# A block inverse from 32-blocks: the three terms of a float16 pair stacked along the contraction

## The chip, the cores and the metric

The kernel runs on one core of a Trainium2 chip. The metric is the device time of one execution in microseconds (us). TensorE (PE) multiplies matrices and writes to PSUM; VectorE (DVE), ScalarE (ACT) and GpSimd (POOL) work element by element; SyncE (SP) issues most DMA transfers, in the order of its own queue. Each engine takes its instructions in a fixed order, which is set when the kernel is compiled.

## The reference

One layer of a hybrid backbone for 2048 sample tokens and 128 context tokens with D = 1024. Three branches work on one input projection; the change lies in the first, a gated delta rule in both directions. Cut to what matters:

```python
def gated_delta_chunked(q, k, v, g, beta, s0):
    ...
    m = eye + bc[..., :, None] * jnp.einsum('bnhik,bnhjk->bnhij', kc, kc) * dec_strict
    rhs = jnp.concatenate([vc * bc[..., None], kc * (bc * jnp.exp(gam))[..., None]], axis=-1)
    sol = lax.linalg.triangular_solve(m, rhs, left_side=True, lower=True, unit_diagonal=True)
    ...
    def step(s, inp):
        u0_, w_, qk_, qg_, kd_, gl_ = inp
        u = u0_ - jnp.einsum('bhck,bhkv->bhcv', w_, s)
        o = jnp.einsum('bhck,bhkv->bhcv', qg_, s) + jnp.einsum('bhij,bhjv->bhiv', qk_, u)
        s = gl_[..., None, None] * s + jnp.einsum('bhck,bhcv->bhkv', kd_, u)
        return s, o
```

The other two branches (a spatial gating unit and a Fourier mix), the gates, the merge and the output projection are matrix products around it. The result holds the tokens of both groups and the final states of the context.

## The kernel before

**Numbers.** Float32 values are held as pairs of float16, a high and a low part. A product of two pairs takes three matmuls, high by high, high by low and low by high (`mm3`, L163; each goes through `mm`, L160, so almost every matmul of the profile stands at L161).

**Chunks.** The kernel uses chunks of 128 tokens, 17 of them: chunk 16 is the context, 0 to 15 the sample. For each chunk, direction and head (H = 4) a unit triangular matrix of 128 by 128 is inverted. `prep` (L652) makes the products of a chunk: it reads the rows of q, k and v (`rows`, tiles kq and qr; one chunk ahead), normalizes them (`norm`: squares on ACT, a scale and a power on POOL), and writes the off-diagonal matrix `n16` as a pair to DRAM (`nD`), and its four diagonal blocks of 32 by 32 through POOL copies (L712) to `ndD`. Stores are issued one step late (`late`).

**Inverses of the 32-blocks.** `base_inverse` (L736) inverts the diagonal blocks of four chunks (a group) at once, by 31 steps on DVE (L759, L760), and writes each inverse and its transpose side by side as float32 to `eD` (L770).

**From 32 to 128.** `level` (L777) is run once for each of the 17 chunks in each direction, 34 times. It loads `n` (tile sn) and the inverses (tile e), splits the inverses to float16 pairs (`ec`, L790 and L791) and spreads them over block-diagonal tiles R16 (the inverse) and T16 (its transpose) with a mask on POOL (L797). Then two levels of block products follow: n times T16, masked (`q32`, L808) and split to Q; Q with R16 and R16 with Q; the results go to R16 and T16 with minus signs (L824 to L830); n times T16 again (L834, mask L837), then Q with R16 (L843). Each of the five products has three terms for four heads, 12 matmuls, 60 in all. Almost all use 128 rows and columns of the array, with zeros in most blocks.

**The scan.** `scan_dir` (L878) runs the chunks of one direction in order; each step needs R of its chunk, which `level` of that chunk makes during the step before. Both are generators. `attend` gives a chunk's output and `finish` the second direction's.

**The order.** The matmuls of the other branches and of the merge are the main program; after each block `Pace.tick` runs some steps of the delta generator (`delta`, L996), by a quota of time per step (QUOTA 1.6, in the scan SCAN 2.7). At the end of the second merge the rest is drained (L1327). A scheduler then orders the instructions of each engine.

**Weights.** Projection weights come in blocks of 128 columns (`wlist`). `fetch` and `weight_step` (L260 to L281) read them and convert them to pairs, some steps per tick; `getw(n, ahead)` gives the next and asks for the following.

The lines that load and spread a level's operands:

```python
        e32 = sb(dq, [P, H, 2, 32], "e32")
        SY.dma_start(e32.rearrange("p h w c -> p h (w c)"), eD[g][d, :, ci])
        ...
        for which, dst in ((0, R16), (1, T16)):
            for l in range(2):
                G.tensor_tensor(dst[:, l].rearrange("p h a b c -> p h (a b) c"), wide(ec[:, :, which ^ d, l, :]), bm, ALU.mult)
```

Of the kernel before, what the change touches and what calls it, by code (L numbers as in the profile page):

```python
# [20 lines left out]
P = 128  # L21
# [90 lines left out]
def hybrid_flow_kernel(ctx: ExitStack, tc: tile.TileContext, x_prompt, x_sample, state_delta, c, c_ctx, ln_g, w_ada,  # L112
# [56 lines left out]
    def rsqrt(out, ss, mul, w):  # L169
        G.tensor_scalar(out, ss, mul, EPS, ALU.mult, ALU.add)  # L170
        G.tensor_tensor(out, out, mhalf.to_broadcast([P, w]), ALU.pow)

    def scales(ss, pl, tag):

        ps = bank(ps_x, [P, 1])
        sb16 = sb(pl, [P, 1], tag + "b", BF16)
        V.tensor_copy(sb16, ss)  # L177
        mm(ps, ones16, sb16)
# [16 lines left out]
    def converting(w, st, nkt, cols=P, hi=None, lo=None, tag="w", bufs=5):  # L195
# [12 lines left out]
        s, inv = scales(ss, wp, "wsc")  # L208
# [43 lines left out]
    v4, vfilled = [], [0]  # L252
    wdone, wnext, wread, wlate, bwp, wsteps = [], [0], [], [0], [], []

    def read_next():
        if len(wread) < min(len(wdone) + 2, len(wlist)):
            src, nkt, tag, bufs = wlist[len(wread)]
            wread.append(read_w(src, nkt))

    def weight_step():  # L260

        if wsteps:
            if next(wsteps[0], 1):
                wsteps.pop(0)
                wlate[0] = 3
        else:
            wlate[0] -= 1
            if wlate[0] <= 0:
                read_next()

    def fetch(upto):
        while len(wdone) < min(upto, len(wlist)):
            src, nkt, tag, bufs = wlist[len(wdone)]
            if tag == "b" and not bwp:
                return
            if len(wread) == len(wdone):
                while wsteps:
                    weight_step()
                read_next()
            wdone.append(_W())  # L280
            wsteps.append(converting(wdone[-1], wread[len(wdone) - 1], nkt, tag=tag, bufs=bufs))  # L281
# [127 lines left out]
    with tc.issue_after(last_ada.ins):  # L409
        fetch(2)  # L410
# [174 lines left out]
    for ct in range(12):  # L585
        w = getw(1, 2)
# [40 lines left out]
    eD = [dram(f"ei{g}", [2, P, len(ts), H, 64]) for g, ts in enumerate(GROUPS)]  # L627
# [10 lines left out]
    def rows(part, t):  # L638
        x = sb(d2, [P, H, P], "kq" if part else "qr", bufs=3 if part else 1)
# [5 lines left out]
    def late(dst, src):  # L645

        if owed:
            SY.dma_start(*owed.pop())
        if dst is not None:
            owed.append((dst, src))  # L650

    def prep(g, ci, t, nxt, held):  # L652
# [11 lines left out]
        def norm(ps, i):  # L664
# [3 lines left out]
            G.tensor_scalar(ss[:, i, :], ss[:, i, :], EPS, None, ALU.add)  # L668
# [10 lines left out]
        yield 1  # L679
        A.activation(tok[:, 1, :], turned(2), AF.Copy, scale=us)  # L680
# [18 lines left out]
        more(0, lambda: rows(0, nxt))  # L699
# [7 lines left out]
        for d in range(2):  # L707
# [3 lines left out]
            for B in range(4):  # L711
                G.tensor_copy(nd[32 * B:32 * B + 32, d], h3(n_)[32 * B:32 * B + 32, :, 32 * B:32 * B + 32])  # L712
# [3 lines left out]
            late(nD[d][t], n16)  # L716
# [19 lines left out]
    def base_inverse(g):  # L736
# [26 lines left out]
        both = XB.rearrange("p (j w c) -> p j w c", j=32, w=2)  # L763
        V.tensor_copy(both[:, :, 1, :], E.rearrange("p (i j) -> p j i", j=32))
        A.copy(both[:, :, 0, :], b3(E))
        yield 1
        for d in range(2):
            for B in range(4):
                p0_ = d * 64 + B * 16
                SY.dma_start(eD[g][d, 32 * B:32 * B + 32].rearrange("j t h c -> (t h) j c"),  # L770
                             both[p0_:p0_ + nb].rearrange("p j w c -> p j (w c)"))
# [3 lines left out]
    odd = [False]  # L775

    def level(d, t):  # L777
        odd[0] = not odd[0]
        ps_l = ps_x if odd[0] else ps_lev
# [6 lines left out]
        R16 = sb(dq, [P, 2, H, 2, 2, 32], "R16", F16, bufs=2)  # L786
        R = R16.rearrange("p l h a b c -> p l (h a b c)")
        yield R
        ec = sb(dq, [P, H, 2, 2, 32], "ec", F16)
        A.activation(ec[:, :, :, 0, :], e32, AF.Copy, scale=FS)  # L790
        V.scalar_tensor_tensor(ec[:, :, :, 1, :], e32, FS, ec[:, :, :, 0, :], ALU.mult, ALU.subtract)  # L791
        T16 = sb(dq, [P, 2, H, 2, 2, 32], "T16", F16, bufs=2)
        bm = K["bm"].rearrange("p (o b x) -> p o b x", o=1, x=1).to_broadcast([P, H, 4, 32])
        wide = lambda t_: t_.rearrange("p h (o c) -> p h o c", o=1).to_broadcast([P, H, 4, 32])
        for which, dst in ((0, R16), (1, T16)):
            for l in range(2):
                G.tensor_tensor(dst[:, l].rearrange("p h a b c -> p h (a b) c"), wide(ec[:, :, which ^ d, l, :]), bm, ALU.mult)  # L797
        yield R
        b0 = d
        nl = lambda h: (n_[:, 0, hs(h)], n_[:, 1, hs(h)])  # L800
        sub = lambda t_, h, b: (t_[:, 0, h, :, b, :], t_[:, 1, h, :, b, :])
        ps = bank(ps_l, [P, H, 64])
        for h in range(H):
            mm3(ps[:, h].rearrange("p (a c) -> p a c", a=2), nl(h), sub(T16, h, b0))
        Q = sb(dq, [P, 2, H, 64], "Q", F16, bufs=2)
        m1 = K["m1f" if d == 0 else "m1b"].rearrange("p (o a x) -> p o a x", o=1, x=1).to_broadcast([P, H, 2, 32])
        f = sb(dq, [P, H, 64], "q32", bufs=2)
        V.tensor_tensor(f.rearrange("p h (a c) -> p h a c", a=2), ps.rearrange("p h (a c) -> p h a c", a=2), m1, ALU.mult)  # L808
        A.activation(Q[:, 0], f, AF.Copy, scale=1.0 / FS)
        V.scalar_tensor_tensor(Q[:, 1], f, 1.0 / FS, Q[:, 0], ALU.mult, ALU.subtract)  # L810
        yield R
        ps12 = bank(ps_l, [P, 2, H, 2, 32])
        ps1, ps2 = ps12[0:64, 0], ps12[:, 1]
# [4 lines left out]
        yield R  # L818
        a0 = d
        rows = lambda a, b: slice(64 * a + 32 * b, 64 * a + 32 * b + 32)  # L820
        for a in (1 - a0, a0):
            ra = rows(a, b0)
            src = ps1[32 * a:32 * a + 32, :, a, :]
            A.activation(R16[ra, 0, :, a, 1 - b0, :], src, AF.Copy, scale=-1.0 / FS)  # L824
            V.scalar_tensor_tensor(R16[ra, 1, :, a, 1 - b0, :], src, -1.0 / FS, R16[ra, 0, :, a, 1 - b0, :], ALU.mult, ALU.subtract)
        a = a0
        ra = rows(a, 1 - b0)
        src = ps2[ra, :, a, :]
        A.activation(T16[ra, 0, :, a, b0, :], src, AF.Copy, scale=-1.0 / FS)
        V.scalar_tensor_tensor(T16[ra, 1, :, a, b0, :], src, -1.0 / FS, T16[ra, 0, :, a, b0, :], ALU.mult, ALU.subtract)  # L830
        half = lambda t_, h, a_: (t_[:, 0, h, a_].rearrange("p b c -> p (b c)"), t_[:, 1, h, a_].rearrange("p b c -> p (b c)"))
        ps = bank(ps_l, [P, H, 64])
        for h in range(H):
            mm3(ps[:, h], nl(h), half(T16, h, a0))  # L834
        Q = sb(dq, [P, 2, H, 64], "Q", F16, bufs=2)
        f = sb(dq, [P, H, 64], "q32", bufs=2)
        V.tensor_scalar(f, ps, K["m2f" if d == 0 else "m2b"], None, ALU.mult)  # L837
        A.activation(Q[:, 0], f, AF.Copy, scale=1.0 / FS)
        V.scalar_tensor_tensor(Q[:, 1], f, 1.0 / FS, Q[:, 0], ALU.mult, ALU.subtract)
        yield R  # L840
        ps = bank(ps_l, [64, H, 64])
        for h in range(H):
            mm3(ps[:, h], (Q[:, 0, h, :], Q[:, 1, h, :]), half(R16, h, 1 - a0))  # L843
        top = [R16[64 * a0:64 * a0 + 64, l, :, 1 - a0].rearrange("p h b c -> p h (b c)") for l in range(2)]
        A.activation(top[0], ps, AF.Copy, scale=-1.0 / FS)
        V.scalar_tensor_tensor(top[1], ps, -1.0 / FS, top[0], ALU.mult, ALU.subtract)
        yield R

# [29 lines left out]
    def scan_dir(d):  # L878
        order = [16] + (list(range(16)) if d == 0 else list(range(15, -1, -1)))
        lev = level(d, order[0])  # L880
        R = next(lev)
        for _ in range(5):
            yield 1
        for R in lev:
            yield 1
            yield 1
        S = S16 = held = None
        for s_, t in enumerate(order):
            nlev = level(d, order[s_ + 1]) if s_ < 16 else iter(())
            R2 = next(nlev, None)  # L890
# [21 lines left out]
            if held is not None:  # L912
                yield from attend(d, *held)
# [543 lines left out]
```

## Time and profile before

| | |
|---|---|
| time, median of three runs | 2273.56 us (2272.32 to 2273.77) |
| the profiled execution | 2270.88 us, of which span 2269.1 us |
| mean granted clock of TensorE | 0.992 |
| instructions in the span | 43042 |
| HBM read / written | 220.46 MB / 127.62 MB |
| chunks prepared, about | 420 to 930 us |
| scan of both directions, about | 930 to 1830 us |

The profile is one execution. "Busy" is the time in which an engine works; a group of instructions stands as line, engine, operation, output and inputs by name, shape, count, then busy time, mean of one in ns, and the idle time ahead of it with what ended most of it. For matmuls the shape begins with rows * columns of the array that hold the stationary operand; the mean of one is from its start to its modelled end, and as they are pipelined they start much closer together than that. PEld is the loading of stationary operands, SPq the issuing of transfers by SP.

### The profile page before, as it was taken

The numbers are of one execution on the slowest core, as the hardware profiler recorded it, in microseconds if no ns is written. First come the engines' busy times: TensorE is split into PE (matmuls) and PEld (weight loads), VectorE is DVE, ScalarE is ACT, GpSimd is POOL, SyncE is SP. The second block draws the span as 40 slices with busy tenths as digits, with TensorE's granted clock in tenths as the row PEclk, the third lists the DMA queues.
The fourth block names the chain that finished last, engine by engine and source line by source line (L and its number), as shares of the span: only waits on it lengthen the run. The fifth ranks groups of instructions, "written<-read, shape, count | busy, mean of one in ns | idle before, by whom it ended". The sixth has DMA issues, their size and how long they took to land.

```text
span 2269.1 us, 43042 instructions
## 1 busy us (share of the span) xinstructions
PE 2190.0 (97%) x16646; PEld 1263.7 (56%) x16646; DVE 1354.3 (60%) x3088; ACT 963.6 (42%) x2181; POOL 834.7 (37%) x988
## 2 busy tenths in 40 slices
PE   7999999899998999999899999999999999999998
PEld 3564444455554588787456555566655444444443
DVE  5637744478859687466756555767666443433454
ACT  3544644443444453344534334655544432222232
POOL 1421432245445432343233323455544211221643
PEclk9999999999999999999999999999999999999999
DMA  8425632375776752433644434665554543333542
GB/s 274 157 74 190 239 110 66 115 223 181 240 221 196 211 174 70 109 102 112 203 133 150 127 125 137 200 194 159 186 163 147 177 146 113 113 120 95 185 149 102
DMA packets 311847, 350.90 MB, mean 155 GB/s; under 512 B 52945, under 2 KB 227002, under 8 KB 309594
## 3 DMA queue, kind: packets, MB, share of 16 engines
q1 hardware_dynamic: 296778, 287.97, 41.4%
q0 software_dynamic: 12416, 51.27, 6.2%
q10 hardware_dynamic: 2448, 8.91, 1.0%
q8 instruction: 130, 2.13, 0.4%
q14 instruction: 75, 0.61, 0.1%
HBM read 220.46 MB, written 127.62 MB: 153 GB/s over the span
## 4 chain that ended last, share of the span: by engine, by line
PE 51%; DVE 6%; DMA 5%; ACT 2%; issue 2%; POOL 2%; SPq 1%; DVEq 0%; POOLq 0%; ACTq 0%
PE b L161 50%; DMA st<-br 2%; DMA wst<-in_w_in_dram 1%; DVE E L760 1%; DVE XB L759 1%; DMA S<-in_state_delta_dram 0%; DVE big L1251 0%; DVE sg L361 0%; POOL st L1051 0%; ACT big L1250 0%; DMA xr<-in_x_sample_dram 0%; DMA wst<-in_w_ada_dram 0%; SPq L770 0%; DMA mrow<-mrg 0%; DMA mrg<-mrow 0%
## 5 line engine op out<-in xcount | busy, mean ns | idle before, releaser
L161 PE MATMUL b<-xh,whi 128*128 128x512 f16 (+1 forms) x1920 | 649.8, 347 | 8.1 <-DVE sg L1289 3.5
L161 PE MATMUL b<-xl,whi 128*128 128x512 f16 (+1 forms) x1920 | 650.4, 348 | 0.0
L161 PE MATMUL b<-xh,wlo 128*128 128x512 f16 (+1 forms) x1920 | 649.6, 348 | 0.0
L161 PEld LDWEIGHTS <-whi 128*128 128x128 f16 x3904 | 360.2, 98 | 345.8 <-issue 13.7
L161 PEld LDWEIGHTS <-wlo 128*128 128x128 f16 x1952 | 191.1, 98 | 175.5 <-issue 2.0
L161 PE MATMUL b<-big,bhi 128*128 128x512 f16 (+1 forms) x960 | 251.2, 347 | 2.0 <-ACT big L1250 1.7
L1290 POOL TENSOR_TENSOR mrow<-mrow,sg 128x512 f32<-128x512 f32 (+1 forms) x80 | 94.7, 1185 | 290.5 <-DVE sg L1289 168.4
L161 PE MATMUL b<-big,blo 128*128 128x512 f16 (+1 forms) x480 | 163.1, 347 | 0.0
L797 POOL TENSOR_TENSOR R<-ec,cst 128x512 f16<-128x512 f16 x68 | 75.1, 1123 | 178.3 <-PE b L161 175.9
L1280 ACT ACTIVATE sg<-b,winv 128x512 f32<-128x512 f32 (+1 forms) x120 | 74.3, 619 | 155.2 <-PE b L161 154.3
L607 POOL TENSOR_TENSOR cy<-cy,raw 128x545 f32<-128x545 f32 (+1 forms) x48 | 67.3, 1427 | 196.2 <-ACT raw L606 196.2
L161 PEld LDWEIGHTS <-xh 128*128 128x128 f16 x1496 | 118.5, 99 | 32.2 <-issue 6.6
L161 PEld LDWEIGHTS <-bhi 128*128 128x128 f16 x960 | 89.5, 98 | 84.2 <-issue 1.0
L1289 DVE SCALAR_TENSOR_TENSOR sg<-b,binv,sg 128x512 f32<-128x512 f32 (+1 forms) x80 | 53.4, 668 | 117.3 <-PE b L161 112.9
L797 POOL TENSOR_TENSOR T<-ec,cst 128x512 f16<-128x512 f16 x68 | 77.8, 1160 | 56.0 <-PE b L161 40.6
L161 PE MATMUL b<-wlo,xh 128*128 128x128 f16 x544 | 94.0, 221 | 0.0
L161 PE MATMUL b<-whi,xh 128*128 128x128 f16 x544 | 94.0, 220 | 0.0
L161 PE MATMUL b<-whi,xl 128*128 128x128 f16 x544 | 93.9, 220 | 0.0
L161 PE MATMUL b<-wohi,mh 128*128 128x512 f16 x240 | 90.9, 379 | 2.0 <-ACT mh L1357 2.0
L206 ACT ACTIVATE wlo<-wst 128x1024 f16<-128x1024 f32 x52 | 55.0, 1057 | 88.2 <-DMA wst<-in_w_in_dram 85.7
L213 DVE SCALAR_TENSOR_TENSOR wlo<-wst,wsc,whi 128x1024 f16<-128x1024 f32 x52 | 70.8, 1366 | 35.3 <-ACT whi L212 34.2
L161 PE MATMUL b<-wohi,ml 128*128 128x512 f16 x240 | 90.8, 379 | 0.3 <-DVE mscb L177 0.3
(442 smaller groups left out, 4427.5 us busy)
## 6 DMA issues: line engine op xcount, KB each, us to landing
wst<-in_w_in_dram SPq DMA_DIRECT2D x60, 512.0 KB
qkv<-cy POOLq DMA_DIRECT2D x12, 1089.0 KB, 5.2
st<-br SPq DMA_DIRECT2D x48, 256.0 KB
mrow<-mrg SPq DMA_DIRECT2D x18, 512.0 KB
mrow<-mrg SPq DMA_DIRECT2D x16, 576.0 KB
mrg<-mrow POOLq DMA_DIRECT2D x16, 576.0 KB, 3.5
dc<-dec SPq DMA_DIRECT2D x17, 512.0 KB
kq<-qkv SPq DMA_DIRECT2D x34, 256.0 KB
```

What stands on the lines that cost most here:

```text
L161: PE.matmul(out, l, r, start=start, stop=stop)
L206: A.activation(w.lo, st, AF.Square, accum_out=ss)
L213: V.scalar_tensor_tensor(w.lo, st, s, w.hi, ALU.mult, ALU.subtract)
L607: G.tensor_tensor(y[:, c0:c1], y[:, c0:c1], raw[:, 1 + c0:1 + c1], ALU.mult)
L759: V.tensor_tensor(t3, X3[:, 0:k, k:k + 1].to_broadcast([P, k, n_]), E3[:, k:k + 1, k:32].to_broadcast([P, k, n_]), ALU.mult)
L760: V.tensor_tensor(E3[:, 0:k, k:32], E3[:, 0:k, k:32], t3, ALU.subtract)
L797: G.tensor_tensor(dst[:, l].rearrange("p h a b c -> p h (a b) c"), wide(ec[:, :, which ^ d, l, :]), bm, ALU.mult)
L1280: A.activation(sg, ps, AF.Sigmoid, scale=gw.inv)
L1289: V.scalar_tensor_tensor(sg, ps, binv[:, 1:2], sg, ALU.mult, ALU.mult)
L1290: G.tensor_tensor(mr, mr, sg, ALU.add)
```

## The change

Inverses of the 32-blocks are turned into float16 pairs once, in `base_inverse`, and written in two layouts: `eD` (pieces of 32 numbers, high and low apart) and `fD` (high and low beside each other). `prep` stores, beside `n16`, the off-diagonal blocks that the first product needs (`nbD`). `level` loads these into tiles in which the three terms of a pair product lie under each other along the contraction (N3 and ES, 3 × 32 = 96 rows: high, high, low against high, low, high), and loads the diagonal blocks of R16 and T16 straight into place; zeros elsewhere are written once for a buffer and direction. The first two products become one matmul per block (8, then 4 and 4); the other two keep three terms, with 64 rows and columns in place of 128 (12 and 12). The scan runs both directions as one loop, and a level's loads are issued one step earlier. The core of `level`:

```diff
-        n_ = sb(dq, [P, 2, WB], "sn", F16, bufs=2)
-        SY.dma_start(n_, nD[d][t])
-        e32 = sb(dq, [P, H, 2, 32], "e32")
-        SY.dma_start(e32.rearrange("p h w c -> p h (w c)"), eD[g][d, :, ci])
...
+        if was != d:
+            G.memset(R16.rearrange("p h l b c -> p (h l b c)"), 0.0)
+            G.memset(T16.rearrange("p h l b c -> p (h l b c)"), 0.0)
+            wide16[k][2] = d
...
+        N3 = sb(dq, [96, 2, H, 32], "N3", F16, bufs=2)
+        ES = sb(dq, [96, 2, 2, H, 32], "ES", F16, bufs=2)
+        for i in range(3):
+            gi = slice(32 * i, 32 * i + 32)
+            SY.dma_start(N3[gi].rearrange("p a h c -> p a (h c)"), nbD[d][t][:, :, i // 2])
+            for which in range(2):
+                src = eD[g][d, (b0 ^ which):4:2, (1 - which) ^ d, :, i % 2, ci].rearrange("a j x -> j a x")
+                SY.dma_start(ES[gi, which].rearrange("p a h c -> p a (h c)"), src)
+        SY.dma_start(n_[first], nD[d][t][first])
+        for b in range(2):
+            SY.dma_start(hl(T16[rows(a0, b)], b), fi(2 * a0 + b, 1))
+        for B in range(4):
+            SY.dma_start(hl(R16[32 * B:32 * B + 32], B), fi(B, 0))
+        yield R16
+        ps = bank(ps_l, [32, H, 2, 32])
         for h in range(H):
-            mm3(ps[:, h].rearrange("p (a c) -> p a c", a=2), nl(h), sub(T16, h, b0))
...
+            for a in range(2):
+                mm(ps[:, h, a], N3[:, a, h], ES[:, 0, a, h])
+        Q3 = sb(dq, [96, H, 2, 32], "Q3", F16)
+        A.activation(Q3[0:32], ps, AF.Copy, scale=1.0 / FS)
+        V.scalar_tensor_tensor(Q3[64:96], ps, 1.0 / FS, Q3[0:32], ALU.mult, ALU.subtract)
+        A.activation(Q3[32:64], ps, AF.Copy, scale=1.0 / FS)
...
         for h in range(H):
-            mm3(ps1[:, h], (Q[:, 0, h, :], Q[:, 1, h, :]), sub(R16, h, 1 - b0))
+            mm(ps2[:, h], ES[:, 1, a0, h], Q3[:, h, a0])
         for h in range(H):
-            mm3(ps2[:, h].rearrange("p a c -> p (a c)"), [R16[:, l, h].rearrange("p a b c -> p (a b c)") for l in range(2)], (Q[:, 0, h, :], Q[:, 1, h, :]))
+            mm(ps1[:, h], Q3[:, h].rearrange("p a c -> p (a c)"), ES[:, 1, :, h])
...
-            mm3(ps[:, h], nl(h), half(T16, h, a0))
...
+            mm3(ps[:, h], [n_[first, l, c0:c0 + 64] for l in range(2)], [T16[first, h, l] for l in range(2)])
...
-            mm3(ps[:, h], (Q[:, 0, h, :], Q[:, 1, h, :]), half(R16, h, 1 - a0))
+            mm3(ps[:, h], [Q[second, l, h] for l in range(2)], [R16[second, h, l, half] for l in range(2)])
```

In `base_inverse` and `prep` (and `norm`):

```diff
-        both = XB.rearrange("p (j w c) -> p j w c", j=32, w=2)
-        V.tensor_copy(both[:, :, 1, :], E.rearrange("p (i j) -> p j i", j=32))
-        A.copy(both[:, :, 0, :], b3(E))
+        both = XB.bitcast(F16).rearrange("p (w j l c) -> p w j l c", w=2, j=32, l=2)
+        A.activation(both[:, 0, :, 0, :], E3, AF.Copy, scale=FS)
+        V.scalar_tensor_tensor(both[:, 0, :, 1, :], E3, FS, both[:, 0, :, 0, :], ALU.mult, ALU.subtract)
+        yield 1
+        for l in range(2):
+            A.copy(both[:, 1, :, l, :], both[:, 0, :, l, :].rearrange("p i j -> p j i"))
...
-                SY.dma_start(eD[g][d, 32 * B:32 * B + 32].rearrange("j t h c -> (t h) j c"),
-                             both[p0_:p0_ + nb].rearrange("p j w c -> p j (w c)"))
+                SY.dma_start(eD[g][d, B].rearrange("w j l t (h c) -> (t h) (w j l) c", c=32),
+                             both[p0_:p0_ + nb].rearrange("p w j l c -> p (w j l) c"))
+                SY.dma_start(fD[g][d, B].rearrange("w j t (h l) c -> (t h) (w j) (l c)", l=2),
+                             both[p0_:p0_ + nb].rearrange("p w j l c -> p (w j) (l c)"))
...
-                G.tensor_copy(nd[32 * B:32 * B + 32, d], h3(n_)[32 * B:32 * B + 32, :, 32 * B:32 * B + 32])
+                A.copy(nd[32 * B:32 * B + 32, d], h3(n_)[32 * B:32 * B + 32, :, 32 * B:32 * B + 32])
...
-            late(nD[d][t], n16)
+            side = [nD[d][t], n16]
+            for a in range(2):
+                m0, i0 = 64 * a + 32 * d, 64 * a + 32 * (1 - d)
+                side += [nbD[d][t][:, a].rearrange("m l (h c) -> m (l h) c", c=32),
+                         n16[m0:m0 + 32].rearrange("p l (h x) -> p (l h) x", h=H)[:, :, i0:i0 + 32]]
+            late(*side)
...
-            G.tensor_scalar(ss[:, i, :], ss[:, i, :], EPS, None, ALU.add)
+            V.tensor_scalar(ss[:, i, :], ss[:, i, :], EPS, None, ALU.add)
```

The same move from POOL to DVE is made in `rsqrt` (L170). Around these: q's rows have two buffers and are asked for earlier; a weight's conversion has a pause more for the first weights, at most one weight is converted at a time, begun by `weight_step` itself, and the next is read after two ticks instead of three; and in the first projection

```diff
-    w = getw(1, 2)
+    w = getw(1, 2 if ct < 6 else min(4, 15 - ct))
```

In the scan, with the level's generator for two steps on:

```diff
+            olev, nlev = nlev, level(*order[i_ + 2][::2]) if i_ < 32 else iter(())
+            R3 = next(nlev, None)
             yield 1
...
-                next(nlev, None)
+                next(olev, None)
                 yield 1
-            for _ in nlev:
+            for _ in olev:
                 pass
...
-    for d in range(2):
-        yield from scan_dir(d)
+    yield from scan()
```

More of the change, by code (lines that the diff above doesn't have):

```diff
@@ L643, in hybrid_flow_kernel, with late @@
     owed = []
[L645 to L650, printed above, removed]
+    def late(*pairs):
+        while owed:
+            SY.dma_start(*owed.pop(0))
+        for i in range(0, len(pairs), 2):
+            owed.append(pairs[i:i + 2])
     def prep(g, ci, t, nxt, held):
@@ L679, in prep @@
         yield 1
+        more(0, lambda: rows(0, nxt))
         A.activation(tok[:, 1, :], turned(2), AF.Copy, scale=us)
@@ L849, in hybrid_flow_kernel @@
+        V.scalar_tensor_tensor(Q[second, 1], src, 1.0 / FS, Q[second, 0], ALU.mult, ALU.subtract)
+        yield R16
+        ps = bank(ps_l, [64, H, 2, 32])
+        half = slice(2 - 2 * a0, 4 - 2 * a0)
+        for h in range(H):
+            mm3(ps[:, h], [Q[second, l, h] for l in range(2)], [R16[second, h, l, half] for l in range(2)])
+        negated(*[R16[first, :, l, half] for l in range(2)], ps)
+        yield R16
     pair = lambda t_, h: (t_[:, 0, hs(h)], t_[:, 1, hs(h)])
@@ L876, in attend, with scan @@
             yield 1
-    def scan_dir(d):
-        order = [16] + (list(range(16)) if d == 0 else list(range(15, -1, -1)))
-        lev = level(d, order[0])
+    def scan():
+        order = [(d, s_, t) for d in range(2) for s_, t in enumerate([16] + (list(range(16)) if d == 0 else list(range(15, -1, -1))))]
+        lev = level(0, 16)
         R = next(lev)
+        nlev = level(*order[1][::2])
+        R2 = next(nlev)
         for _ in range(5):
             yield 1
-        for R in lev:
+        for _ in lev:
             yield 1
             yield 1
[L887 to L890, printed above, removed]
+        held = None
+        for i_, (d, s_, t) in enumerate(order):
+            if s_ == 0:
+                S = S16 = None
             kT_ = sb(dq, [P, 2, WB], "sk", F16)
@@ L912, in scan_dir @@
             if held is not None:
-                yield from attend(d, *held)
+                yield from attend(*held)
             qk_ = sb(dq, [P, 2, WB], "sqk", F16)
```

150 lines of the change are left out of this document (65 added, 85 removed).

## Prediction

> **What bounds the kernel now.** I read the page's engine line first, then the busy times by stage, the waits of TensorE (PE) in each, the tiles of the changed code, and last the timeline and the queues where the change works.
>
> ```profile
> PE 2190.0 (97%) x16646; PEld 1263.7 (56%) x16646; DVE 1354.3 (60%) x3088; ACT 963.6 (42%) x2181; POOL 834.7 (37%) x988
> ```
>
> TensorE is busy for 2190.0 of 2269.1 us; 79 us are idle. No other engine passes 60%. So the change can win in two ways only: a shorter matmul stream, or fewer of the 79 us. By stage (columns: time, PE, weight loads, DVE, ACT, POOL, clock, DMA share, GB/s):
>
> ```profile
> 420.00:930.00 510.00, 481.40 (x3771) 310.06 (x3769) 368.96 (x943) 217.28 (x617) 217.37 (x363) 0.99 0.63 185
> 930.00:1830.00 900.00, 875.68 (x8235) 547.16 (x8236) 570.58 (x1378) 425.05 (x1066) 352.21 (x334) 0.99 0.47 151
> ```
>
> The preparation of the chunks (420 to 930) leaves TensorE idle for 28.6 us, the scan (930 to 1830) for 24.3 us. Both stages are touched. TensorE's waits in the first and in the second of them, in total, times, longest:
>
> ```profile
> PE b L693 <- DVE tok L678: 7.3, 5, 3.4
> PE b L161 <- DVE T L695: 6.7, 7, 1.6
> PE b L161 <- ACT v4hi L212: 4.2, 1, 4.2
> ...
> PE b L161 <- DVE v4lo L213: 1.5, 1, 1.5
> ```
> ```profile
> PE b L161 <- DVE sg L1289: 3.1, 1, 3.1
> PE b L161 <- DVE T L830: 3.0, 3, 2.5
> PE b L161 <- ACT Q L838: 2.2, 1, 2.2
> ...
> PE b L161 <- ACT R L845: 1.3, 1, 1.3
> ```
>
> No wait is long. What the change does to the stream therefore decides first.
>
> **The matmul stream of a level.** In the trace of before, a level's 60 products stand in three of the groups below (sn and T, R and Q twice); v with R is the scan's own product with the finished inverse:
>
> ```profile
> L161 PE MATMUL b<-R,Q 128*64 128x64 f16 x816 | 48.3, 200 | 2.3 <-ACT Q L838 2.2
> L161 PE MATMUL b<-T,sn 128*128 128x64 f16 x816 | 42.6, 194 | 3.1 <-DVE T L830 3.0
> ...
> L161 PE MATMUL b<-v,R 128*128 128x128 f16 x408 | 32.7, 219 | 4.7 <-ACT v L852 2.0 <-ACT R L845 1.3 <-DVE R L846 0.9
> ...
> L161 PE MATMUL b<-Q,R 128*128 128x64 f16 x408 | 19.5, 194 | 0.0
> ```
>
> The form "128*64" says that 128 rows and 64 columns of the array hold the stationary operand. The mean of one (194 to 200 ns) is a latency; the rate comes from the timeline, where groups follow without a wait (start, duration, count):
>
> ```profile
> 1466.66 0.83 PE L161 MATMUL b<-v,R 128*128 128x128 f16 x12
> 1467.43 0.56 PE L161 MATMUL b<-R,Q 128*64 128x64 f16 x12
> 1467.92 0.52 PE L161 MATMUL b<-Q,R 128*128 128x64 f16 x12
> 1468.28 0.38 PE L161 MATMUL b<-big,bhi 128*128 128x512 f16 x1
> ```
>
> Full width, 64 output columns: (520 − 194) / 11 = 29.6 ns each. Width 64: (560 − 200) / 11 = 32.7 ns. Twelve of the first take 0.355 us, and the next group starts 0.36 us after them: no gap at equal width. Twelve of the second take 0.39 us, yet the next group starts 0.49 us later: leaving width 64 costs 0.10 us. The twelve of the row above run at (830 − 219) / 11 = 55.5 ns, 0.67 us, and the narrow group starts 0.77 us after them: entering costs 0.10 us too.
>
> That is the rule of the Trainium skill, page "TensorEngine Tiling (Array Packing)", section "Tiling Modes", that changing the tiling mode drains the engine; the trace agrees and gives it 0.10 us. It speaks against this change, which uses three new widths.
>
> After, a level has 40 products: eight with 96 rows and width 32 (the first product, three terms in one), four of the same width and four with width 64 (the second), and 24 of 64 rows and width 64. Those shapes are not in the trace. Nearest, for the narrow ones, is the interleaved pair of 16 and 32 output columns:
>
> ```profile
> 159.00:165.00 6.00, 6.00 (x239) 0.00 (x0) 0.00 (x0) 1.00 0.13 51
> ```
>
> 6.00 us / 239 = 25 ns each. I take 25 ns for width 32 and 32.7 ns for the others. Bounds: 25 ns for all; at the top 32.7 ns for width 32 and 55.5 ns (128 columns' rate) for 64 rows. Over 34 levels:
> - before: 1224 × 29.6 + 816 × 32.7 = 62.9 us;
> - after: 408 × 25 + 952 × 32.7 = 41.3 us (34 to 63 us).
>
> Now the changes of width. In the compiled order of the matmuls, the used rows or columns change 261 times before and 465 times after: each of four groups enters and leaves, and the scheduler splits groups by other work. 204 more at 0.10 us add 20.4 us. If the 33 steps from width 32 to 64 inside the second product were free, it would be 17; no row suggests a dearer change. Sum of the stream: −21.6 + 20.4 = −1 us (−12 to +21). The third of the products that goes is paid back in changes of width.
>
> **What else leaves, and what covers it.** POOL no longer spreads the blocks nor copies the diagonal blocks:
>
> ```profile
> L797 POOL TENSOR_TENSOR T<-ec,cst 128x512 f16<-128x512 f16 x68 | 77.8, 1160 | 56.0 <-PE b L161 40.6 <-ACT ec L790 10.3 <-DVE big L1251 3.2
> L797 POOL TENSOR_TENSOR R<-ec,cst 128x512 f16<-128x512 f16 x68 | 75.1, 1123 | 178.3 <-PE b L161 175.9 <-ACT ec L790 2.0 <-DVE ec L791 0.4
> ...
> L712 POOL COPY nd<-n 32x128 f32<-32x128 f32 x136 | 63.5, 467 | 42.5 <-DVE n L710 37.4
> ```
> ```profile
> L791 DVE SCALAR_TENSOR_TENSOR ec<-e,ec 128x256 f16<-128x256 f32 x34 | 26.7, 784 | 6.5 <-ACT ec L790 6.3
> ```
>
> POOL loses 153 us in the scan and 63 in the preparation, DVE 27 us and two mask steps a level in the scan, while ACT, 43% busy in the preparation, gains the 136 small copies. All lies beside TensorE and is worth only what waits. In the scan the chain of a level loses the split (0.8 us on DVE), four spreads (1.1 us each) and the mask steps, its loads go out a whole chunk earlier, and its last two stages no longer run back to back. The waits on T L830, Q L838 and R L845 are 6.5 us; I take half, 3.3. In the preparation, eight copies (8 × 0.47 us a chunk) no longer stand ahead of the power step (L669) that tok L678 needs, but that step's input now comes from DVE, 72% busy there (369 of 510 us): half of 7.3, 3.6 us, and nothing of T L695. The last weights before the V stage are fetched up to four ahead instead of two: the v4 waits, 5.7 us, mostly go (4). The scan has 17 pauses fewer, and in the compiled order its last products stand some 40 us of branch matmuls earlier, clear of the drain at the end of the second merge, where sg L1289 held TensorE for 3.1 us: 2 us. Moving the first scaling step of each inverse root to DVE hides under TensorE, and in the tail it is one small step on either engine: 0. Sum of the idle time: −13 us; bounds 0 and −23 (all of these waits: 6.5 + 7.3 + 5.7 + 3.1 = 22.6).
>
> **What the DMA queue gets.** SP issues 1526 transfers instead of 942. Inverses now go out in pieces of 64 and 128 bytes; before in pieces of 256. The two nearest bursts, each by the queue's own row over its window (733 to 742 us for the inverses going out, 868 to 874 for the blocks of 128 bytes coming in) and by SP's:
>
> ```profile
> q1 hardware_dynamic: 3747, 0.94, 68.6%
> ```
> ```profile
> q1 hardware_dynamic: 3770, 0.60, 58.2%
> ```
> ```profile
> 732.63 8.48 SPq L770 DMA_DIRECT2D ei<-XB  x8
> ...
> 747.38 0.39 SPq L640 DMA_DIRECT2D kq<-qkv  x1
> ```
>
> 3747 packets in 68.6% of 16 × 9 us are 26.4 ns each; 3770 in 58.2% of 16 × 6 us are 14.8 ns. A group of four chunks wrote 4096 packets, 26.4 × 4096 / 16 = 6.8 us; it will write 16,384 of 64 and 8192 of 128 bytes: at 14.8 ns 22.7 us, at 26.4 ns 40.6 us. I take 14.8, as size falls. The 68 diagonal-block stores of the preparation (256 pieces of 64 bytes each) add 16 us of queue time over 510 us at a DMA share of 0.63: covered. The row after the burst is what queues behind it: the next chunk's k rows, issued at 747.38 and read by TensorE at 767.82.
>
> ```profile
> 767.82 0.60 PE L661 MATMUL b<-cst,kq 128*128 128x128 f32 x4
> ```
>
> 20 us of slack cover 16 us more, so 0; without cover 14 us per full group. In the scan a level's 16 loads take SP about 16 × 0.39 = 6 us of the 26 us that a chunk lasts (900 / 34), and each may hold weights and rows behind it while it waits for TensorE to release R; they are issued more than a chunk ahead, so 0 again; bound +6, once, where the scan begins and nothing is loaded yet.
>
> The page "DMA: Bandwidth & Descriptors" of the Trainium skill, section "Specifications", sets 512 bytes as the least for line rate, with a read-modify-write below. Here 128-byte packets were cheaper each, if dearer per byte; writes of 64 bytes are shown by no row, and that rule is behind the second rival.
>
> **Sum.** −1 − 13 = −14 us on an execution of 2270.9 us (span 2269.1 and 1.8 around it), 2.7 us under the median 2273.6. Forecast: 2259 us.
>
> **The rivals.**
> - Even: the stream costs what it did and the idle time only moves to other waits, for SP's in-order queue and DVE. For: 942 to 1526 transfers, DVE busier than POOL in the preparation. Against: fewer stages. 2272 us.
> - The inverse's small writes hold SP's queue. From 18 ns a packet (20 us of slack plus 6.8 us, × 16 / 24,576) the k rows come late; at 26.4 ns each of three groups stalls 14 us and the scan's first product, whose operands pass through the last group's burst, as much: 4 × 14 = 56, half caught by k rows that already lie in their three buffers: +28 − 14, 2287 us. Against: 14.8 ns at 128 bytes.
> - 64 rows cost 55.5 ns: +22 on the stream, 2281 us. For: half the array idles, and nothing shows that shape. Against: width 64 costs 32.7 ns, near the full 29.6.
> - Better: products of 25 ns (−7) and all named waits gone (−10 more): 2242 us. For: POOL off both chains.
>
> **How the numbers follow.** Forecast 0.52, better 0.15, even 0.13, small writes 0.12, dear rows 0.08. A measurement tells 0.2% (4.5 us) from no change. Faster: 0.50 + 0.15 + 0.04 = 0.69; same: 0.02 + 0.09 + 0.02 = 0.13; slower 0.18. The range takes in "better" with 2 us more and most of the small writes' case: 2240 to 2284; the forecast's own range is 2248 to 2270.
>
> **What would show it.** Right: 1360 products in narrow forms at 25 to 33 ns, steps of 0.10 us at each change of width, the sum of both within a few us of before; L797's rows gone; PE busy near 2190 less a few us and idle near 65; no wait of TensorE on kq or N3 above a few us. Wrong: 64*64 products over 45 ns apart, the inverse's SP rows over 30 us a group, or waits on sv, v or R grown in the scan.

## The result, and the profile after

Median of the changed kernel: 2362.48 us (2354.69 to 2364.19), against 2273.66 us (2272.32 to 2274.41) before, four runs each: ratio 1.0385 with a 95% interval of 1.0361 to 1.0408. It is slower by 89 us, far outside the forecast range. The profiled execution took 2364.19 us (span 2362.0, clock 0.970 where it was 0.992).

From the page of the changed kernel: engines, then the chain of waits by engine and by line.

```profile
PE 2206.9 (93%) x15966; PEld 1257.3 (53%) x15966; DVE 1286.4 (54%) x3076; ACT 1018.5 (43%) x2327; POOL 599.8 (25%) x634
...
PE 51%; SPq 6%; DVE 5%; DMA 3%; ACT 2%; issue 1%; POOL 0%; DVEq 0%; POOLq 0%; ACTq 0%
PE b L161 50%; SPq L791 3%; DVE E L776 1%; DVE XB L775 1%; SPq L789 1%; SPq L825 1%; ACT XB L784 0%; DVE n L721 0%; DMA st<-br 0%; SPq L765 0%; DMA wst<-in_w_in_dram 0%; PE b L997 0%; DMA ES<-ei 0%; DMA mrow<-mrg 0%; DMA nb<-n 0%
```

TensorE is busy 17 us more and idle 155.1 us instead of 79.1: 76 + 17 = 93 us, the whole difference of the spans. L791 and L789, SP's issues of the inverses' writes, stand on the chain. By stage, with the columns of the prediction's table:

```profile
420.00:930.00 510.00, 420.47 (x2896) 254.36 (x2894) 322.41 (x849) 234.88 (x689) 122.03 (x156) 0.92 0.66 175
930.00:1830.00 900.00, 859.75 (x7888) 550.19 (x7889) 495.37 (x1302) 423.88 (x1068) 190.77 (x187) 0.97 0.51 146
```

In the preparation TensorE is idle 89.5 us where it was 28.6, it does 2896 matmuls where it did 3771, and its granted clock is 0.92 instead of 0.99. So the loss begins there; by 930 the kernel is already behind, and the start of the scan falls into the second row. TensorE's waits in the two stretches (total, times, longest):

```profile
PE b L705 <- DVE tok L689: 21.2, 3, 18.9
PE b L705 <- ACT sq L678: 20.3, 1, 20.3
PE b L161 <- DVE vrow L1156: 11.1, 1, 11.1
PE b L672 <- DMA kq<-qkv: 5.1, 1, 5.1
```
```profile
PE b L161 <- DVE yT L1231: 17.9, 1, 17.9
PE b L161 <- ACT xc L1200: 15.3, 1, 15.3
PE b L161 <- DVE xc L1188: 5.6, 1, 5.6
```

Before, no wait in either stretch was above 4.2 us. Now five are between 11 and 20 us, under five different names. Their common cause is on SP's queue. Its timeline across one group of four chunks (start, duration; each group has eight of both writes):

```profile
789.15 0.32 SPq L789 DMA_DIRECT2D ei<-XB  x1
789.52 2.93 SPq L791 DMA_DIRECT2D fi<-XB  x1
792.55 0.52 SPq L651 DMA_DIRECT2D kq<-qkv  x1
793.11 1.35 SPq L789 DMA_DIRECT2D ei<-XB  x1
794.52 3.71 SPq L791 DMA_DIRECT2D fi<-XB  x1
...
818.54 0.56 SPq L789 DMA_DIRECT2D ei<-XB  x1
819.15 3.73 SPq L791 DMA_DIRECT2D fi<-XB  x1
822.97 0.51 SPq L651 DMA_DIRECT2D kq<-qkv  x1
```

The sixteen writes, with one load of k rows between them, hold the queue from 789.15 to 822.88, 33.7 us; the eight writes of before took 8.48. There are five groups, and with each comes one of the long waits:

| the group's writes, us | TensorE waits until | for | us |
|---|---|---|---|
| 556 to 598 (chunk 16 alone) | 586 | vrow | 11.1 |
| 669 to 705 | 714 | tok | 18.9 |
| 789 to 823 | 836 | sq | 20.3 |
| 893 to 926 | 934 | yT | 17.9 |
| 997 to 1029 | 1039 | xc | 15.3 |

The first group is one chunk, with a quarter of the pieces, yet its issues take SP 25.2 us where the others take 31.0 to 32.4 (before: 6.6 where the others took 6.3 to 8.2). So the time doesn't go by the number of pieces in all; what is the same in all five is the number of pieces for each row of the source.

How such a stretch reaches TensorE is seen at the fourth (in brackets: idle time before, and what ended it):

```profile
922.65 3.57 SPq L791 DMA_DIRECT2D fi<-XB  x1
926.32 0.49 SPq L659 DMA_DIRECT2D n<-n  x1
926.86 2.23 SPq L659 DMA_DIRECT2D nb<-n  x2
```
```profile
931.41 0.63 ACT L742 ACTIVATE n<-n 128x512 f16<-128x512 f32 x1 [23.00 <-DMA nb<-n]
```
```profile
934.03 0.29 PE L161 MATMUL b<-whi,xh 128*128 128x128 f16 x1 [17.95 <-DVE yT L1231]
```

The stores of `n16` and of its blocks beside the diagonal go out only behind the last write; until they have landed, ACT can't write their buffers (three of them) again, sits for 23.00 us with everything queued behind it, DVE waits for ACT, and TensorE stands for 17.95 us. The second and the third wait come the same way: ACT sits at L742 for 12.99 and 22.78 us. The first goes through vrow, which is read back from memory that the stores of vs wrote, both issued between the writes. The fifth goes through POOL:

```profile
1032.63 0.95 POOL L811 MEMSET R<- 128x1024 f16 x1 [26.36 <-DMA fi<-XB]
```
```profile
1036.65 0.63 ACT L1080 ACTIVATE sg<-st 128x512 f32<-128x512 f32 x1 [24.57 <-POOL st L1079]
```

The clearing of R, which is new in this change, waits on POOL until the last writes have landed (the tile lies in a pool that is opened only then, perhaps in the memory that XB gave back; no run shows it); `st` stands behind it, ACT waits for `st`, and TensorE for ACT.

The matmul stream came out as forecast. Rows of the scan (start, duration, count), and the groups with their mean:

```profile
1110.56 0.56 PE L161 MATMUL b<-T,sn 64*64 64x64 f16 x12
1111.06 0.23 PE L161 MATMUL b<-whi,xh 128*128 128x128 f16 x1
...
1186.99 0.35 PE L161 MATMUL b<-ES,N 96*32 96x32 f16 x8
```
```profile
L161 PE MATMUL b<-T,sn 64*64 64x64 f16 x408 | 26.3, 199 | 5.9 <-ACT T L852 4.2 <-DMA ES<-ei 1.6
...
L161 PE MATMUL b<-ES,N 96*32 96x32 f16 x272 | 13.2, 178 | 0.1
```

(560 − 199) / 11 = 32.8 ns for 64 rows, (350 − 178) / 7 = 24.6 ns for width 32. Twelve of the first take 0.39 us, and the next group starts 0.50 us after them: a change of width costs the 0.10 us forecast here too. In the traces the used rows or columns change 263 times before and 467 times after.

Where the 17 us more of busy time come from is in the clock. Windows of the changed kernel through the third wait, from 816.1 to 836.4 (columns as above):

```profile
814.00:816.00 2.00, 2.00 (x16) 1.39 (x13) 0.00 (x0) 0.00 (x0) 0.00 (x0) 1.00 0.52 62
816.00:820.00 4.00, 0.11 (x2) 0.00 (x0) 0.00 (x0) 0.00 (x0) 0.00 (x0) 0.83 0.62 72
...
836.00:838.00 2.00, 1.63 (x12) 1.60 (x13) 0.88 (x2) 0.86 (x5) 1.21 (x2) 0.50 0.51 68
838.00:840.00 2.00, 2.00 (x28) 2.00 (x27) 0.00 (x0) 0.50 (x2) 0.65 (x1) 0.71 1.10 316
840.00:842.00 2.00, 1.84 (x33) 1.72 (x31) 0.00 (x0) 2.00 (x6) 0.00 (x0) 1.00 1.27 211
```

The grant falls to half some 2.5 us into the stall and stays there for about 3 us after work is back, so a stall goes on costing after its end. By the trace's records of the clock, TensorE worked 68.9 us at half clock (before: 26.8 us); taking half of that as lost gives 34.5 us against 13.4. Busy time less this loss is 2172.4 us after and 2176.6 before. So the sum is: idle +76, clock +21, stream −4, together +93.

The Trainium skill states on its page "TensorE: Matmul & The Clock Gate", section "Part 1: The HAM clock gate", that an idle window of about 3.4 us halves the clock and a busy one gives it back. The trace agrees on the length: stretches at half clock last 3.41 us or a multiple of it (3.41, 6.83, up to 20.48), but for the one that the end of the kernel cuts short. It doesn't agree that the window must be idle: this stretch begins at 818.67 us, and in the 3.41 us before that TensorE was still busy for 0.85 us. The prediction had no price for the half clock.

### The profile page after: what moved, and what is told of

The parts are those of the page before. It is cut to its first block, busy times and chain, and to the rows that moved or that the text cites. A ratio compares the mean times of both kernels' runs of the same rounds, so it can differ in the third digit from the quotient of the medians.

```text
span 2362.0 us, 42181 instructions
## 1 busy us (share of the span) xinstructions
PE 2206.9 (93%) x15966; PEld 1257.3 (53%) x15966; DVE 1286.4 (54%) x3076; ACT 1018.5 (43%) x2327; POOL 599.8 (25%) x634
## 4 chain that ended last, share of the span: by engine, by line
PE 51%; SPq 6%; DVE 5%; DMA 3%; ACT 2%; issue 1%; POOL 0%; DVEq 0%; POOLq 0%; ACTq 0%
PE b L161 50%; SPq L791 3%; DVE E L776 1%; DVE XB L775 1%; SPq L789 1%; SPq L825 1%; ACT XB L784 0%; DVE n L721 0%; DMA st<-br 0%; SPq L765 0%; DMA wst<-in_w_in_dram 0%; PE b L997 0%; DMA ES<-ei 0%; DMA mrow<-mrg 0%; DMA nb<-n 0%
## 5 line engine op out<-in xcount | busy, mean ns | idle before, releaser
L161 PE MATMUL b<-xh,whi 128*128 128x512 f16 (+1 forms) x1920 | 655.6, 350 | 13.1 <-DVE vrow L1156 11.1
L175 DVE CAST wscb<-wss 128x1 bf16<-128x1 f32 x93 | 14.2, 154 | 204.6 <-ACT wlo L209 99.6
L616 POOL TENSOR_TENSOR cy<-cy,raw 128x545 f32<-128x545 f32 (+1 forms) x48 | 74.3, 1575 | 184.1 <-ACT raw L615 184.1
L161 PE MATMUL b<-whi,xh 128*128 128x128 f16 x544 | 95.5, 223 | 17.9 <-DVE yT L1231 17.9
L928 POOL TENSOR_TENSOR kn<-skn,kn 128x512 f16<-128x512 f32 x34 | 40.3, 1184 | 258.2 <-ACT kn L927 258.1
```

The lines of the kernel that those rows point to most:

```text
L161: PE.matmul(out, l, r, start=start, stop=stop)
L616: G.tensor_tensor(y[:, c0:c1], y[:, c0:c1], raw[:, 1 + c0:1 + c1], ALU.mult)
L928: G.tensor_tensor(kn16[:, 1, :], kn_, kn16[:, 0, :], ALU.subtract)
```

## The experiments

All ratios are against the kernel before, run beside on the same chip; its median was 2277.38 us beside e1, e2, e3 and e5, 2278.40 beside e6, e8, e9 and e10, and 2279.55 beside e11, e15, e17 and e18. e1, e2 and e3 have two runs each, e8 ten, the others four. Theory: the burst of small writes costs it all. Rivals: the other edits, the level's loads, DMA bandwidth.

**e1: one of the two layouts.** The inverses are written in the first layout alone, and R and T come from it, one half of the pairs at a time (22 loads a level instead of 16):

```diff
-                SY.dma_start(fD[g][d, B].rearrange(...), both[...])
+        for l in range(2):
+            for b in range(2):
+                SY.dma_start(T16[rows(a0, b), :, l, b], fi(2 * a0 + b, 1, l))
+            for B in range(4):
+                SY.dma_start(R16[32 * B:32 * B + 32, :, l, B], fi(B, 0, l))
```

> The changed kernel without the second layout fD: R16 and T16 are loaded from eD, high and low in two transfers (22 loads a level in place of 16). The output is the same. Theory 'queue' (the inverses' small writes hold SP's in-order queue for some 36 us per group; the stores of the preparation queued behind keep their buffers, and ACT, DVE and in the end TensorE wait for those buffers): a group's writes fall from 24,576 to 16,384 packets and from 16 to 8 transfers, the burst to 10 to 20 us, and the time to 2275 to 2310 us. Rival 'other edits' (scaling steps on DVE, diagonal copies on ACT, weights converted one at a time): 2345 to 2365 us, as the changed kernel.

Measured: 2312.55 us, ratio 1.0148 (1.0117 to 1.0180). The eight writes of 16,384 pieces last 18 to 22 us a group. The time is 2.5 us past the range of the theory and far from the rivals': most of the loss goes with part of the burst.

**e2: the writes on POOL's queue.** `SY.dma_start` of L789 and L791 becomes `G.dma_start`.

> The changed kernel with the inverses' writes (eD and fD) issued from POOL's queue in place of SP's; the same packets. Theory 'queue': SP is free, the stores leave in time, 2265 to 2300 us, unless POOL needs over 3 us to issue one and then holds what stands behind on POOL. Rival 'bandwidth' (the many small packets slow every other transfer, whichever queue they come from): 2340 us or more. Rival 'other edits': 2345 to 2365 us.

Measured: 2318.34 us, 1.0174 (1.0136 to 1.0211), between the two. SP's queue is free of the burst now, but slow all the same:

```profile
560.65 7.70 SPq L749 DMA_DIRECT2D dc<-dec  x1
568.44 1.46 SPq L659 DMA_DIRECT2D qT<-q  x1
570.00 2.11 SPq L659 DMA_DIRECT2D qk<-n  x1
572.20 7.50 SPq L1110 DMA_DIRECT2D vs<-vs  x1
```

A load that takes 0.4 us to issue takes 7.7 while POOL's small pieces are under way. This fits the rule of the Trainium skill, page "DMA: Bandwidth & Descriptors", section "Issuing engines are not separate DMA queues": all queues end on the same DMA engines, and another issuer saves issue time only. Here another issuer saved half the loss; the other half stayed. Not all of that half need be SP's: POOL now sits on the writes itself. Between 554.8 and 586.5 us it waits 6.27, 3.85 and 4.62 us for writes of its own to land before it goes on, and the power step that follows (L680) comes behind them. No run separates the two.

**e3: the burst added to the kernel before.** Same writes, same pieces, from the same tile to memory that nothing reads:

```diff
+                SY.dma_start(xD[g][d, B].rearrange("w j l t (h c) -> (t h) (w j l) c", c=16), ...)
+                SY.dma_start(yD[g][d, B].rearrange("w j t (h l) c -> (t h) (w j) (l c)", l=2), ...)
```

> The kernel before, which also writes its inverses to two scratch tensors nobody reads, in the same pieces (128 pieces of 64 bytes and 64 of 128 bytes per row), counts and order as the changed kernel. Nothing else changes. Theory 'queue': the burst alone costs most of the loss, 2330 to 2370 us. Rival 'other edits' and rival 'level' (the new products and loads of the scan): under 2290 us.

Measured: 2405.98 us, 1.0558 (1.0521 to 1.0596): 129 us, more than the whole change loses and 36 us above the theory's range, with the old levels and none of the other edits. The old eight writes stand in the burst as well, and a group's 24 transfers take 38 to 50 us, so this isn't the burst of the change alone; that it is dear without any of the rivals' edits is shown.

**e5: whole rows.** Each partition's inverses go out as one row of 8 KB; the loads gather them in pieces of 64 bytes, 28 loads a level instead of 16:

```diff
+                SY.dma_start(eD[g][d, B].rearrange("t h w j l c -> (t h) (w j l c)"),
+                             both[p0_:p0_ + nb].rearrange("p w j l c -> p (w j l c)"))
```

> The changed kernel with each inverse written once, a whole row of 8 KB per partition (8 writes of 16 packets a group); the level gathers the blocks from it, 28 loads a level in pieces of 64 bytes. The output is the same. Theory 'queue': the burst is gone, TensorE's idle time in the preparation returns to about 30 us or less; the stream is even, so 2255 to 2275 us, plus what 12 more loads a level cost SP in the scan (28 x 0.47 = 13 of 26 us a chunk: nothing if covered). Rival 'other edits': 2345 us or more. Rival 'level': the scan's idle time stays at 50 us or more, 2285 us or more.

Measured: 2295.51 us, 1.0086 (1.0054 to 1.0117). The preparation is cured, the scan isn't:

```profile
420.00:930.00 510.00, 491.19 (x3929) 321.77 (x3927) 375.49 (x984) 270.78 (x763) 139.60 (x181) 0.99 0.63 183
930.00:1830.00 900.00, 857.42 (x7245) 515.40 (x7243) 475.62 (x1250) 409.35 (x1038) 190.09 (x179) 0.98 0.53 148
```

18.8 us idle in the first (28.6 before the change), 42.6 in the second (24.3). The time is 20 us above the theory's range and in that of the rival 'level', so something in the scan still cost.

**e6: pauses in the burst.** `yield 1` twice after each pair of writes.

> The changed kernel with two pauses of the interleaver after each pair of inverse writes, so that a group's eight pairs go out over a longer stretch with other work's stores and loads between them; bytes, pieces and issues are the same. If it is the unbroken stretch on SP's queue that holds up stores and, through their buffers, ACT: 2290 to 2325 us. If the time that SP needs for the issues counts however it is laid out: 2350 to 2370. If the longer way of the last group's blocks into the scan takes over: above 2370.

Measured: 2404.93 us, 1.0558 (1.0536 to 1.0581). The edit didn't do what it should: in the trace the sixteen writes still follow one another, in 35 to 47 us a group, and the last group ends at 1093 instead of 1029 us. The time lies in the range of the third case, the longer way into the scan, and the late end fits it, though that this is the cause isn't shown; on the first two cases the run says nothing.

**e8, e9, e10: what is left in e5.** e8 is e5 with the twelve ES loads of a level on POOL's queue. e9 is the kernel before with the small edits alone (weights fetched and converted one at a time, first scaling steps and the norms' addition on DVE, diagonal blocks copied on ACT, q rows earlier). e10 is e5 without them.

> Whole rows (inverses written once, in rows of 8 KB), with the twelve ES loads of a level issued by POOL's queue instead of SP's. Theory A, that the rest of 20 us comes from a level's 28 loads on SP: 2262 to 2280 us. Theory B, that it comes from the other edits (weights, scaling steps and small copies moved between engines): 2292 to 2305.

> The kernel before with only the small edits: weight fetching and its conversion one at a time, the first scaling step of each inverse root and the addition in the norms on DVE, the diagonal blocks' copies on ACT, two q row buffers fetched earlier. Levels and inverses as before. Theory A (level's loads): 2262 to 2276 us. Theory B (these edits): 2290 to 2300.

> Whole rows with the small edits undone, so that the new levels and the inverses' rows stand alone. Theory A (level's loads): 2285 to 2300 us. Theory B (small edits): 2262 to 2278.

Measured: e8 2281.73 us, 1.0018 (0.9998 to 1.0038); e9 2266.10 us, 0.9942 (0.9925 to 0.9960); e10 2297.14 us, 1.0085 (1.0057 to 1.0113). The small edits cost nothing, they win 12 us; in the presence of 28 loads that gain is gone. Theory A, the loads, holds in e9 and e10; e8 lies 2 us past its range, 10 us short of the other's. In e8 the loads that left SP cost POOL 0.55 us each (POOL is busy for 418 us of the scan's 900, in the changed kernel for 191), so e8 isn't free of its own cost.

**e17, e18: whole rows with fewer loads.** The blocks are laid down in another order, so that two ES loads become one, and T's pairs lie side by side: 20 loads on SP. e18 moves its six ES loads to POOL: 14 on SP.

```diff
-    eD = [dram(f"ei{g}", [2, 4, len(ts), H, 2, 32, 2, 32], F16) ...
+    eD = [dram(f"ei{g}", [2, 2, len(ts), H, 2, 2, 32, 2, 32], F16) ...
...
+                src = eD[g][d, b0 ^ which, ci, :, :, (1 - which) ^ d, :, i % 2].rearrange("h a j c -> j (h a) c")
+                SY.dma_start(ES[gi, which].rearrange("p h a c -> p (h a) c"), src)
```

> Whole rows again (inverses written once, no burst of small pieces), laid out so that a level takes 20 loads on SP's queue instead of 28 (the change has 16). Theory A, that the number of loads on SP's queue sets what is left of the loss: 2274 to 2288 us, between the run with 28 and the one with 16 there. Theory B, that the count on SP doesn't matter and POOL's queue helped for another reason: 2288 to 2302.

> The same, with the six ES loads of a level issued by POOL: 14 loads on SP, six on POOL instead of twelve. Theory A: 2255 to 2276 us, and a share of half-clock time in the scan below that of the run with twelve ES loads on POOL. Theory B, that the new level costs some 15 us in itself (short waits that drop the clock), wherever its loads are issued: 2277 to 2290.

Measured: e17 2263.37 us, 0.9921 (0.9899 to 0.9944); e18 2259.93 us, 0.9910 (0.9887 to 0.9933). Both beat both kernels. e17's page and stages, and its issues of the inverses (shortest, median, longest, ns):

```profile
PE 2189.9 (97%) x15966; PEld 1249.2 (55%) x15966; DVE 1290.5 (57%) x3076; ACT 1017.0 (45%) x2327; POOL 592.6 (26%) x634
```
```profile
420.00:930.00 510.00, 488.93 (x3910) 320.53 (x3909) 375.55 (x984) 270.25 (x763) 141.19 (x181) 0.99 0.63 183
930.00:1830.00 900.00, 874.41 (x7446) 525.10 (x7444) 491.74 (x1291) 421.55 (x1059) 194.33 (x184) 0.99 0.54 152
```
```profile
L788 SPq DMA_DIRECT2D ei<-XB x40: 283/470/976, 554.2 to 909.8; - x40
```

Same products, same edits, four loads a level more than the change, but a write of 0.47 us in place of a pair of 4: idle time 72.7 us, stages at clock 0.99. From 0.9921 to 1.0385 is 4.7%, some 105 us: the price of the burst against whole rows, since the four loads more count against e17. From e5 to e17 eight loads a level, 8 × 0.43 = 3.4 us of SP's time, cost 1.7% (37 us); from 20 to 14, with six on POOL, 3 us within overlapping intervals.

**e11: the preparation's stores on POOL's queue.** In `late`, `SY.dma_start` becomes `G.dma_start`; the burst stays.

> The changed kernel with the preparation's own stores (scaled rows, blocks beside the diagonal, turned rows) on POOL's queue; the burst of inverse writes stays on SP. Theory C, that the burst does its harm by the stores behind it, whose buffers ACT then waits for: 2290 to 2325 us, with the long waits on sq, tok and yT gone. Rival D, that loads behind the burst (rows, weights, blocks to invert) stall the engines just as much: 2340 to 2365.

Measured: 2353.13 us, 1.0319 (1.0300 to 1.0338), the rival's range. The waits that ended with sq and tok are gone, and others stand in their place (TensorE's waits from 420 to 1100; L705 is the same matmul as before, released by another):

```profile
PE b L161 <- DVE vrow L1156: 27.4, 1, 27.4
PE b L705 <- DVE E L776: 22.3, 1, 22.3
PE b L161 <- ACT xc L1200: 16.3, 1, 16.3
PE b L672 <- DMA kq<-qkv: 15.7, 1, 15.7
```
```profile
602.51 1.41 DVE L1156 SCALAR_TENSOR_TENSOR vrow<-b,winv,vrow 128x512 f32<-128x512 f32 x2 [30.62 <-DMA vrow<-vs]
```

DVE sat idle for 30.62 us before vrow landed. That load had to wait for the last store of vs, which isn't among the stores that moved and went out at 593.23 us, right behind the burst's end at 592.64; the load followed at 597.41. kq is a load and nothing else, issued at 826.27 behind a burst that ended at 826.17, and TensorE waits 15.7 us for it. My theory that the preparation's held stores alone do the harm fell: whatever lies behind the burst is late, store or load.

**e15: loads alone.** e9 with 27 loads a level more, of 128 pieces of 64 bytes, into a tile that nothing reads.

> The run with the small edits alone (old levels, old inverses; 0.9942 of the kernel before), with 27 more loads per level on SP's queue, of 128 pieces of 64 bytes, into a tile that nothing reads. Theory A: the issue time alone costs 8 to 20 us, 2272 to 2286. Theory B, that the new levels' own waits cost and not the loads on SP: 2262 to 2270.

Measured: 2362.24 us, 1.0354 (1.0327 to 1.0380), 4.1% over e9; both theories had it far too low. The loads took 0.43 us each:

```profile
L798 SPq DMA_DIRECT2D x<-ei x918: 302/430/1889, 907.7 to 1627.9; - x184
```

27 × 0.43 = 12 us a level, of some 26 us that a chunk lasts. So loads on SP's queue in the scan do cost, and steeply at 28 or 29 a level. The traces say why that may be. From the first of the levels' loads to the last, SP's queue, with the scan's other transfers in it, is taken for 26% of the time before, 66% after, 61% in e18 and 75% in e17, but 92% in e5 and in e10 and 87% in e15 (a gap between one issue and the next counts as free from 0.12 us up). At 28 loads hardly any slack is left on it. In e15 most of the free time, too, is the loads' own doing: they write the same few places again and again and wait for each other (total, times, longest),

```profile
SPq L798 <- DMA x<-ei: 65.4, 92, 2.2
```

so e15 may put the price of loads alone too high. That the full queue is the whole of it isn't shown: in e8 SP is taken for 60%, and it is still 1% above e17. No run separates the queue's order from the engines behind it.

## Why the prediction was wrong

- **The step that failed** is the paragraph on the DMA queue, "20 us of slack cover 16 us more, so 0". Both halves were wrong.
  - The length (16 us more assumed, 25 measured: 33.7 against 8.48): 14.8 ns was the time of the engines per packet, spread over sixteen full engines. But the row it came from, one of loads, shows them 58.2% busy, so 14.8 / 0.582 = 25.4 ns of elapsed time, 39 us a group and not 22.7. The other row, of stores, had its elapsed time in the same fence: eight writes of 4096 pieces in 8.48 us are 33 ns, not 26.4. After, in the stretch shown above, the packets did cost little (60.3% of sixteen engines for 34 us and 25,267 packets, 13 ns each), but the stretch lasted 33.7 × 16 / 24,576 = 22 ns a piece. Both elapsed figures lie above that, and above the 18 ns from which the second rival decides. Over 30 us a group is also the sign of being wrong that the prediction named.
  - The cover: I asked only when the next k rows were needed. A queue in order holds everything behind it, and the prediction's slack belonged to one of its customers. The victims were stores whose buffers were due, vrow, and on POOL the clearing of R; TensorE waited 5.1 us for kq in all.
- **The second rival** (small writes hold SP's queue) named the mechanism and, at 18 ns, the point from which it decides. It was given 0.12 and +28 us; the burst costs about 105. Its price counted three or four stalls of 14 us, half of them caught. There were five, of 11 to 20 us, one of them with the single chunk that it hadn't counted, and the clock added to them.
- **A term was missing:** the half clock after a stall, +21 us here.
- **The stream** was right: 24.6 and 32.8 ns at 25 and 32.7 assumed, 204 changes of width more as counted. The −4 us at −1 forecast says no more than "even": the same figure (busy time less the clock's loss) runs from 2167 to 2178 us over the runs with the new levels. The dear 64 rows didn't happen.
- **The idle time** of −13 us can be judged only without the burst, in e17, which keeps every other edit. Its time fits: 0.9921, 18 us less at this kernel's time where the sum had 14. The waits named went much as forecast or better (tok from 7.3 to 1.6 us, v4 from 5.7 to 0, sg from 3.1 to 0; T, Q and R only from 6.5 to 5.4), but a new one of 9.1 us for xc at the start of the scan took most of it back: by the two profiles idle time fell by 6.4 us. How far the agreement of the total is luck stays open. e9 shows the small edits' part: 12 us, where the steps named for them (tok and the v4 waits) had 3.6 + 4.
- **A level's 16 loads at 0** holds only as far as e17 and e18 reach, at 20 and 14 on SP; "6 us of 26" was no safe argument, as it left out what else the queue carries. The bound "once, where the scan begins" did come: in e17 the first two levels' 40 loads fill SP's queue from 913 to 938 us, ACT waits 14.4 us for a load behind them (skn), and TensorE the 9.1 us for ACT.

## What to carry to other kernels

Price a stretch of transfers by its elapsed time on the queue, from the first issue to the last, not by packet time over all engines; small pieces on the write side that are spread over the memory for the reader's sake can cost more than the reader saves, and here whole rows out with somewhat more loads in was the better bargain. Then list everything that will be queued behind that stretch, stores and the buffers they hold too, and look for the earliest due. Count a stall of TensorE with the slow clock that follows it.

## What was not expected of the hardware

- A write in 1024 pieces of 128 bytes took SP 3.3 us to issue (median of L791) when it followed one in 2048 pieces of 64 bytes that took 0.6, while this queue's packets filled only some 60% of the engines' time (72% with the other queues'):

```profile
q1 hardware_dynamic: 25267, 2.74, 60.3%
```

Its columns are the packets, the MB and the share of sixteen engines of the queue from 789 to 823 us. The issue lasts longer than the packets' own time accounts for.
- With such writes on another queue SP's own issues can be slow all the same: 7.5 and 7.7 us in e2, beside 0.4 otherwise.
- Short waits suffice for the half clock: e8 has no stall above 4.1 us, yet its granted clock over the span is 0.981, against 0.992 before.
